# Sliding-window attention with sinks: a half-block's logits, values and products in a new order, and the low halves of sixteen weight panels on VectorE

## Chip, cores and metric

The kernel runs on one core of a Trainium2 chip. The metric is the device time of one execution in microseconds (us), as the median of several runs on one chip; lower is better. All data are float32. Where a large product is needed, each operand is split into a rounded high half and a low half, and three float32r matmuls (`mm3`: high by high, high by low, low by high) stand for one exact product.

## What is computed

The reference is a four-part network on 512 tokens of width 1024: a gated delta-rule mixer (stage a), attention with a 128-token window and sinks (stage b), a second mixer (stage m), and a product-key expert layer (stage p). The change lies in stage b alone. Cut to it:

```python
def swa_sink_mixer(h, w_in, q_gain, sinks, w_out, k_band, v_band, bias, mask):
    q, z = jnp.split(h @ w_in, 2, axis=-1)
    q = rms_norm(q.reshape(B, T, B_Q_HEADS, B_HD), q_gain) * (B_HD ** -0.5)
    q = q.reshape(B, nb, BLOCK, B_KV_HEADS, B_GROUP, B_HD)
    logits = jnp.einsum("bnqkgd,bnskd->bnkgqs", q, k_band) + bias
    logits = jnp.where(mask[None, :, None, None], logits, -jnp.inf)
    m = jnp.maximum(jnp.max(logits, axis=-1, keepdims=True), sink)
    p = jnp.exp(logits - m)
    probs = p / (jnp.sum(p, axis=-1, keepdims=True) + jnp.exp(sink - m))
    o = jnp.einsum("bnkgqs,bnskd->bnqkgd", probs, v_band)
    o = o.reshape(B, T, B_W) * jax.nn.silu(z)
    return o @ w_out
```

There are 4 key/value heads with 8 query heads each, head width 64, and 4 blocks of 128 tokens; a block of queries sees its own block of keys and the one before.

## The kernel before

Stage b works in four groups `g`, one for each key/value head. In a group, TensorE does two kinds of work.

The **attention** of the group is `block_b(k, s1, s2, g, n, b, ...)` for the four token blocks `n` and three parts `b`. Parts 0 and 1 take four heads each, a half. A half issues its logits (matmuls of line 901 into the PSUM tile `pl`), adds the bias and takes the row extreme on VectorE (line 904, into `lg` and `bm`), exponentiates on ScalarE (910), turns the result by TensorE transposes (917, into the PSUM tile `pt`), copies it to `PT` (919: the first copy of a half on ScalarE, the second on VectorE) and multiplies by the values (922, into `po`). Lines 907, 908 and 911 put the sink into the denominator `bden`. Part 2 divides by the denominators (883, 885), multiplies by the gate on GpSimd (887), turns the result (890) and splits it into `yh` and `yl` (212, 213).

The **projections** are the rest: `gates(g)` (16 steps of six matmuls into `pj`, then lines 805 and 806), the output projection `outputs(g - 1)` (16 steps of six, in the last group eight of twelve, each added to the residual `x` on VectorE, line 821: 56 adds) and `queries(g + 1)` (16 steps of six; after every fourth, `headnorm` makes `qn` on VectorE with lines 307, 206, 186 to 198 and 310, then line 794 turns it and line 795 copies it to `qT`). `weave` sorts the steps of both lists by their place in their own list. A scheduler then sets the order on each engine from this order and its own estimates of when an operand is ready. Every engine takes its instructions strictly in that order.

`Feed` streams the weight panels: a load on SyncE's queue, the high half on ScalarE (line 230 with a gain, 233 without), the low half on VectorE (231, two pieces) where there is a gain. A panel of the output projection (`wbo`, four for each group, 16 in all) has no gain; its low half is line 235, on GpSimd (`lo_on_pool=True`). Stage m has a `Feed` of its own with low halves on GpSimd.

PSUM holds two `pj`, two `pt`, three `pl` and one `po`. `yh` and `yl` have one buffer each: a group's first write to them waits until the output projection of the group before has read the old ones.

Of the kernel before, what the change touches and what calls it, by code (L numbers as in the profile page):

```python
# [7 lines left out]
F32 = mybir.dt.float32  # L8
# [4 lines left out]
AF = mybir.ActivationFunctionType  # L13
ALU = mybir.AluOpType
# [4 lines left out]
P = 128  # L19
T = 512  # L20
NT = 4
# [346 lines left out]
class Feed:  # L368


    def __init__(self, k, srcs, bufs):
        self.k, self.srcs, self.bufs = k, srcs, bufs
        self.raw, self.pans, self.done = [], [], 0

    def load(self, n):
# [5 lines left out]
    def prep(self, n):  # L381
        while len(self.pans) < min(n, len(self.srcs)):
            i = len(self.pans)
            self.load(i + 1)
            self.pans.append(self.k.halves(self.raw[i], bufs=self.bufs, gain=self.srcs[i][1], lo_on_pool=True))
            self.load(i + 3)

    def step(self, n=1):
# [8 lines left out]
def v4(t):  # L397
    return t.rearrange("p (n c) -> p n c", n=NT)
# [339 lines left out]
def stage_b(k):  # L738
    tc, nc, a = k.tc, k.nc, k.a
    with pool(tc, name="sb1", bufs=1) as s1:  # L740
        kT = s1.tile([P, 4, T], F32, name="kT")
# [39 lines left out]
        def queries(g, s2, pt, acc=None):  # L781
            d = gs[g]

            def use(t, p):
                if t == 0:
                    d["bias"] = s2.tile([P, 8, 256], F32, tag="bias", name="bias")
                    nc.sync.dma_start(d["bias"], bass.AP(k.brow.tensor, k.brow.offset + g * 8 * 384, [[1, P], [384, 8], [1, 256]]))
                    d["qT"] = s2.tile([P, 4, T], F32, tag="qT", name="qT", bufs=2)
                qn = s2.tile([P, 8, 64], F32, tag="qn", name="qn")
                k.headnorm(s2, p, qn, 8)  # L790
                q = pt()
                q2 = qn.rearrange("p (m j) c -> p m (j c)", j=2)
# [4 lines left out]
            return tiles_steps(k, feed, at["q", g], tiles, hh, hl, use, acc)  # L797

        def gates(g, s2):
            d = gs[g]  # L800
# [25 lines left out]
        with pool(tc, name="sb2", bufs=1) as s2:  # L826
# [23 lines left out]
                    f()  # L850
            with pool(tc, name="pb", bufs=2, space=PSUM) as k.pb:
                pt = lambda: k.pb.tile([P, 512], F32, tag="pt", name="pt")
                for g in range(4):
                    attend = [lambda n=n, b=b, g=g: block_b(k, s1, s2, g, n, b, gs[g], kT, V, sinkrow) for n in range(NT) for b in range(3)]
                    fill = gates(g, s2)
                    if g:
                        fill += outputs(g - 1, (0, 1), False) + outputs(g - 1, (2, 3), False)
                    if g < 3:
                        fill += queries(g + 1, s2, pt)
                        weave(attend, fill)  # L860
                        continue
                    o = outputs(3, range(4), True)
                    weave(attend[:9], fill)
                    weave(attend[9:], o[:4])
        for _, f in o[4:]:
            f()


def block_b(k, s1, s2, g, n, b, d, kT, V, sinkrow):

    nc = k.nc
    ts = slice(n * P, (n + 1) * P)

    s0, w = (3 - n) * P, P if n == 0 else 2 * P
    nst = w // P
    if b == 0:
        if n == 0:
            d["yh"], d["yl"] = (s1.tile([P, 4, T], F32R, tag=f"y{i}", name=f"y{i}") for i in "hl")
        d["po"] = k.pb.tile([P, 512], F32, tag="pv", name="po", bufs=1)
        d["den"] = k.sm.tile([P, 8], F32, tag="bden", name="bden")  # L880
    po, den = d["po"], d["den"]
    if b == 2:
        nc.vector.reciprocal(den, den)
        o = s2.tile([P, 512], F32, tag="ob", name="ob", bufs=2)
        nc.vector.tensor_tensor(out=o.rearrange("p (h c) -> p h c", h=8), in0=po.rearrange("p (h c) -> p h c", h=8),
                                in1=den.rearrange("p (h o) -> p h o", o=1).to_broadcast([P, 8, 64]), op=ALU.mult)
        nc.gpsimd.tensor_tensor(out=o, in0=o, in1=d["z"][n], op=ALU.mult)
        pt = v4(k.pb.tile([P, 512], F32, tag="pt", name="pt"))
# [3 lines left out]
        return  # L892
    hs = slice(4 * b, 4 * b + 4)
    sk = sinkrow[:, 8 * g + 4 * b : 8 * g + 4 * b + 4]
    lg = s2.tile([P, 4, 256], F32, tag="lg", name="lg", bufs=2)
    m = k.sm.tile([P, 4], F32, tag="bm", name="bm")
    for j in range(2):
        p = k.pb.tile([P, 512], F32, tag="pl", name="pl", bufs=3).rearrange("p (i s) -> p i s", i=2)
        js = slice(64 * j, 64 * j + 64)
        for i in range(2):  # L900
            nc.tensor.matmul(p[:, i, 0:w], d["qT"][js, 2 * b + i, ts], kT[js, g, s0 : s0 + w], start=True, stop=True)
        for i in range(2):
            h = 2 * i + j
            nc.vector.tensor_tensor_reduce(lg[:, h, 0:w], p[:, i, 0:w], d["bias"][:, 4 * b + h, 0:w], 1.0, sk[:, h : h + 1],
                                           ALU.add, ALU.min, m[:, h : h + 1])
    es = k.sm.tile([P, 4], F32, tag="bes", name="bes")
    nc.vector.tensor_tensor(out=es, in0=m, in1=sk, op=ALU.subtract)
    nc.scalar.activation(es, es, AF.Exp)
    for h in range(4):
        nc.scalar.activation(lg[:, h, 0:w], lg[:, h, 0:w], AF.Exp, scale=-1.0, bias=m[:, h : h + 1], accum_out=den[:, 4 * b + h : 4 * b + h + 1])  # L910
    nc.vector.tensor_tensor(out=den[:, hs], in0=den[:, hs], in1=es, op=ALU.add)
    PT = s2.tile([P, 8, P], F32, tag="PT", name="PT", bufs=2)
    for q in range(nst):
        pt = k.pb.tile([P, 512], F32, tag="pt", name="pt")
        for i in range(4):
            h, st = divmod(4 * q + i, nst)
            nc.tensor.transpose(pt[:, i * P : (i + 1) * P], lg[:, h, st * P : (st + 1) * P], k.ident)
        eng = nc.vector.tensor_copy if q else nc.scalar.copy
        eng(PT[:, 4 * q : 4 * q + 4, :], v4(pt))
    for h in range(4):  # L920
        for st in range(nst):
            nc.tensor.matmul(po[:, (4 * b + h) * 64 : (4 * b + h + 1) * 64], PT[:, h * nst + st, :],  # L922
                             V[:, s0 // P + st, g * 64 : (g + 1) * 64], start=(st == 0), stop=(st == nst - 1))

# [761 lines left out]
```

## Time and profile before

| | |
|---|---|
| runs (us) | 2825.43, 2817.9, 2822.9; median 2822.9 |
| profiled execution (us) | 2819.12, its span 2817.4 |
| busy share of the span | PE 95%, DVE 70%, ACT 40%, POOL 30% |
| mean granted TensorE clock | 0.984 |
| attention of stage b, first logits to the last output matmul | 689 to 1101 us of the span |

Engines: PE is TensorE, PEld its weight loads, DVE VectorE, ACT ScalarE, POOL GpSimd, SP SyncE. A matmul's end is modelled, so that matmuls that follow each other closely overlap in the profile: in an undisturbed run of them, one starts every 0.23 us and lasts 0.39 us. A gap shown before a matmul therefore is shorter than the time that PE lost there. "idle before, releaser" names what ended a gap. Line numbers are those of the kernel before.

### The profile page before, as it was taken

How to read it: one execution, taken by the hardware profiler on the slowest of the kernel's cores; microseconds unless marked ns; L12 is line 12 of the kernel's file. 1: busy time of each engine (PE TensorE's matmuls, PEld its weight loads, DVE VectorE, ACT ScalarE, POOL GpSimd, SP SyncE). 2: the span in 40 equal slices, each digit the busy share in tenths (PEclk: the TensorE clock that was granted, in tenths of full speed). 3: DMA queues.
4: the chain of work that ended last, by engine and by line, in shares of the span. 5: the costliest groups of instructions: out<-in, count | busy, mean ns of one | idle time of the engine just before them, and what ended most of it. 6: DMA issues, size and time to landing. Idle time of an engine off the chain costs nothing.

```text
span 2817.4 us, 39316 instructions
## 1 busy us (share of the span) xinstructions
PE 2686.6 (95%) x14291; PEld 2219.0 (79%) x14291; DVE 1966.2 (70%) x4283; ACT 1128.3 (40%) x2304; POOL 839.0 (30%) x609
## 2 busy tenths in 40 slices
PE   7999999989898989899998989899999999999999
PEld 5777777767676767677677788899888888888887
DVE  6566666665655656636646899986777877878886
ACT  5444444434443333333422245564333333333332
POOL 0100000000111032242123247864444444444441
PEclk9999999999999999999999989999999999999999
DMA  4111211121211222121013235557899999898996
GB/s 151 53 53 61 60 61 57 46 70 60 74 61 55 66 68 67 60 68 38 16 53 127 84 127 193 193 185 265 317 324 328 318 326 336 314 321 319 325 325 232
DMA packets 170462, 440.92 MB, mean 157 GB/s; under 512 B 13932, under 2 KB 79756, under 8 KB 168604
## 3 DMA queue, kind: packets, MB, share of 16 engines
q1 hardware_dynamic: 133404, 304.17, 32.8%
q0 software_dynamic: 36864, 134.23, 12.6%
q8 instruction: 113, 1.85, 0.3%
q14 instruction: 81, 0.66, 0.1%
HBM read 401.60 MB, written 36.75 MB: 156 GB/s over the span
## 4 chain that ended last, share of the span: by engine, by line
PE 68%; DVE 16%; issue 6%; ACT 5%; POOL 3%; DMA 2%; SPq 0%; ACTq 0%; DVEq 0%; POOLq 0%
PE pj L315 11%; PE pj L316 11%; PE pj L317 11%; PE acc L316 4%; PE acc L317 4%; PE acc L315 4%; ACT whio L233 2%; PE po L922 2%; PE pG L1644 1%; DVE x L1512 1%; DVE wloo L235 1%; DVE wlo L235 1%; PE po L316 1%; POOL o L1634 1%; PE po L315 1%
## 5 line engine op out<-in xcount | busy, mean ns | idle before, releaser
L315 PE MATMUL pj<-hThi,whi 128*128 128x384 f32 (+2 forms) x1664 | 603.6, 363 | 2.7 <-ACT hg L1390 2.0
L317 PE MATMUL pj<-hThi,wlo 128*128 128x384 f32 (+2 forms) x1664 | 593.5, 357 | 11.9 <-DVE wlo L235 11.9
L316 PE MATMUL pj<-hTlo,whi 128*128 128x384 f32 (+2 forms) x1664 | 598.0, 359 | 0.0
L317 PEld LDWEIGHTS pj<-hThi,wlo 128*128 128x128 f32 x1664 | 317.4, 191 | 33.9 <-DVE wlo L235 12.5
L315 PEld LDWEIGHTS pj<-hThi,whi 128*128 128x128 f32 x1664 | 317.2, 191 | 32.5 <-ACT hg L1390 2.7
L316 PEld LDWEIGHTS pj<-hTlo,whi 128*128 128x128 f32 x1664 | 317.7, 191 | 24.9 <-issue 1.3
L316 PE MATMUL acc<-wloo,Wh 128*128 128x512 f32 x768 | 302.9, 394 | 3.9 <-DVE wloo L235 2.5
L315 PE MATMUL acc<-whio,Wh 128*128 128x512 f32 x768 | 300.9, 392 | 0.5 <-ACT whio L233 0.4
L317 PE MATMUL acc<-whio,Wl 128*128 128x512 f32 x768 | 300.4, 391 | 0.0
L1503 POOL DMA_INDIRECT raw<-in_v_dram,ids x128 | 191.4, 1495 | 236.6 <-DVE wloo L235 114.7
L1503 POOL DMA_INDIRECT raw<-in_u_dram,ids x128 | 185.5, 1449 | 243.7 <-DVE wloo L235 115.0
L235 DVE TENSOR_TENSOR wlo<-raw,whi 128x1024 fp32r<-128x1024 f32 x128 | 161.1, 1258 | 77.8 <-ACT whi L233 77.8
L212 ACT CAST Wh<-W 128x384 fp32r<-128x384 f32 x128 | 65.7, 513 | 369.0 <-DVE W L1450 336.9
L233 ACT CAST whi<-raw 128x1024 fp32r<-128x1024 f32 x144 | 150.2, 1043 | 123.7 <-issue 88.2
L235 DVE TENSOR_TENSOR wloo<-raw,whio 128x1024 fp32r<-128x1024 f32 x128 | 156.8, 1225 | 51.5 <-ACT whio L233 51.5
L235 POOL TENSOR_TENSOR wlo<-wraw,whi 128x1024 fp32r<-128x1024 f32 x52 | 124.5, 2407 | 207.6 <-ACT whi L233 207.5
L316 PEld LDWEIGHTS acc<-wloo,Wh 128*128 128x128 f32 x768 | 144.2, 188 | 44.2 <-DVE wloo L235 16.5
L317 PEld LDWEIGHTS acc<-whio,Wl 128*128 128x128 f32 x768 | 144.2, 188 | 30.5
L315 PEld LDWEIGHTS acc<-whio,Wh 128*128 128x128 f32 x768 | 144.1, 188 | 29.4 <-ACT whio L233 1.4
L1512 DVE SCALAR_TENSOR_TENSOR x<-raw,act,x 128x1024 f32<-128x1024 f32 x128 | 163.8, 1280 | 1.0
L1507 DVE SCALAR_TENSOR_TENSOR raw<-raw,xt 128x1024 f32<-128x1024 f32 x128 | 154.0, 1219 | 0.0
L233 ACT CAST whi<-wraw 128x1024 fp32r<-128x1024 f32 x100 | 104.5, 1048 | 107.0 <-PE pj L316 70.0
(423 smaller groups left out, 5405.9 us busy)
## 6 DMA issues: line engine op xcount, KB each, us to landing
raw<-in_uT_dram SPq DMA_DIRECT2D x128, 512.0 KB
raw<-in_v_dram SPq DMA_DIRECT2D x128, 512.0 KB
wraw<-in_wa_dram SPq DMA_DIRECT2D x48, 512.0 KB
G<-stage SPq DMA_DIRECT2D x12, 2048.0 KB
Gt<-G SPq DMA_DIRECT2D x32, 768.0 KB
wraw<-in_wb_dram SPq DMA_DIRECT2D x32, 512.0 KB
wraw<-in_wmt_dram SPq DMA_DIRECT2D x20, 512.0 KB
H<-hg SPq DMA_DIRECT2D x48, 192.0 KB
```

Of the source, the lines that this page charges most:

```text
L212: self.nc.scalar.copy(hi, src)
L233: nc.scalar.copy(hi, raw)
L235: eng.tensor_tensor(out=lo, in0=raw, in1=hi.bitcast(F32), op=ALU.subtract)
L315: nc.tensor.matmul(out, wh, mh, start=first, stop=False)
L316: nc.tensor.matmul(out, wh, ml, start=False, stop=False)
L317: nc.tensor.matmul(out, wl, mh, start=False, stop=last)
L922: nc.tensor.matmul(po[:, (4 * b + h) * 64 : (4 * b + h + 1) * 64], PT[:, h * nst + st, :], V[:, s0 // P + st, g * 64 : (g + 1) * 64], star ...
L1503: nc.gpsimd.indirect_dma_start(out=g, out_offset=None, in_=src, in_offset=bass.IndirectOffsetOnAxis(ap=ids[:, j : j + 1], axis=0))
L1507: nc.vector.scalar_tensor_tensor(g, g, 1.0, xt0, op0=ALU.mult, op1=ALU.mult, accum_out=act[:, j : j + 1])
L1512: nc.vector.scalar_tensor_tensor(k.x[:, 0, :], g, act[:, j : j + 1], k.x[:, 0, :], op0=ALU.mult, op1=ALU.add)
L1634: nc.gpsimd.tensor_scalar(out=o1[:, n, :], in0=k.c["iota"], scalar1=selT[:, 1, cs][:, n : n + 1], scalar2=None, op0=ALU.is_equal)
L1644: nc.tensor.matmul(p[:, n * P : (n + 1) * P], o1[:, n, :], o0[:, n, :], start=True, stop=True)
```

## The change

Four things change, all in stage b.

1. `block_b` is called once for a group and returns five functions: `logits(u)`, `values(u)`, `products(u)`, `finish(n)` and `turn(n)`, with `u = 2n + b` for the eight halves. `values` is the transposes and copies, `products` the matmuls with the values. The list of attention steps puts `logits(u + 1)` ahead of `values(u)`, a `turn` of the block before between `values(u)` and `products(u)` for even `u`, and `finish` behind the products of odd `u`. Each is a step of its own for `weave`. The last turn of a group goes behind the first logits of the next.
2. In `queries`, the turn of `qn` is a step of its own, two projection steps behind the one that ends its tile; the last one goes into the next group's list.
3. `weave` of the last group is cut at another place: the four last output steps that are woven in lie beside `logits(6)` and what follows it.
4. Stage b's `Feed` gets `lo_on_pool=False`: the 16 low halves of `wbo` move from GpSimd to VectorE.

```diff
-    def __init__(self, k, srcs, bufs):
+    def __init__(self, k, srcs, bufs, lo_on_pool=True):
...
-        feed = Feed(k, srcs + wo(3), 6)
+        feed = Feed(k, srcs + wo(3), 6, lo_on_pool=False)
...
+            steps = []
+            for i, st in enumerate(tiles_steps(k, feed, at["q", g], tiles, hh, hl, use, acc)):
+                steps.append(st)
+                if i > 4 and i % 4 == 1:
+                    steps.append((0.2, lambda t=i // 4 - 1: turn(t)))
+            return steps + [(0.2, lambda: turn(NT - 1))]
...
-                    attend = [lambda n=n, b=b, g=g: block_b(k, s1, s2, g, n, b, gs[g], kT, V, sinkrow) for n in range(NT) for b in range(3)]
+                    L, V_, O_, F, T_ = block_b(k, s1, s2, g, gs[g], kT, V, sinkrow)
+                    attend = [lambda L=L: L(0)] + left
+                    for u in range(8):
+                        if u < 7:
+                            attend.append(lambda L=L, u=u: L(u + 1))
+                        attend.append(lambda V_=V_, u=u: V_(u))
+                        if u % 2 == 0 and u:
+                            attend.append(lambda T_=T_, u=u: T_(u // 2 - 1))
+                            if u == 4:
+                                cut = len(attend) + 1
+                        attend.append(lambda O_=O_, u=u: O_(u))
+                        if u % 2:
+                            attend.append(lambda F=F, u=u: F(u // 2))
+                    left = [lambda T_=T_: T_(NT - 1)]
...
                     if g < 3:
-                        fill += queries(g + 1, s2, pt)
-                        weave(attend, fill)
+                        qs = queries(g + 1, s2, pt)
+                        left.append(qs[-1][1])
+                        weave(attend, fill + qs[:-1])
                         continue
                     o = outputs(3, range(4), True)
-                    weave(attend[:9], fill)
-                    weave(attend[9:], o[:4])
+                    weave(attend[:cut], fill)
+                    weave(attend[cut:] + left, o[:4])
```

The arithmetic inside the five functions is that of before. In the changed kernel the lines are: logits 920 (was 901), bias and row extreme 923 (904), the denominator 926, 927 and 930 (907, 908, 911), exponentials 929 (910), transposes 940 (917), copies 942 (919), products 951 (922), division 956 and 958 (883, 885), gate 960 (887), turn 966 (890), query turn 797 (794), residual 830 (821).

What the scheduler makes of it shows at three places. The first is TensorE in group 0, at the first half of block 2. Before, its logits are `pl_6606` and `pl_6611`, and the exponentials of the same half (`lg_6604`) are turned five projection matmuls later:

```order
L901 MATMUL pl_6606<-kT_5592,qT_6067 128x256 x2
L901 MATMUL pl_6611<-kT_5592,qT_6067 128x256 x2
L315 MATMUL pj_6595<-whi_6267,hThi_5597 128x512
L316 MATMUL pj_6595<-wlo_6268,hThi_5597 128x512
L317 MATMUL pj_6595<-whi_6267,hTlo_5598 128x512
L315 MATMUL pj_6595<-whi_6267,hThi_5597 128x512
L316 MATMUL pj_6595<-wlo_6268,hThi_5597 128x512
L917 MATMUL pt_6625<-cst_71,lg_6604 128x128 x2
```

Now, `pl_6715` and `pl_6720` are the logits of the half after, and the transposes behind them read `lg_6616`, whose own logits were issued 30 projection matmuls, the eight transposes and the products of another half, and two turns earlier:

```order
L920 MATMUL pl_6715<-kT_5592,qT_6067 128x256 x2
L920 MATMUL pl_6720<-kT_5592,qT_6067 128x256 x2
L315 MATMUL pj_6705<-whi_6261,hThi_5597 128x512
L316 MATMUL pj_6705<-wlo_6262,hThi_5597 128x512
L317 MATMUL pj_6705<-whi_6261,hTlo_5598 128x512
L315 MATMUL pj_6705<-whi_6261,hThi_5597 128x512
L316 MATMUL pj_6705<-wlo_6262,hThi_5597 128x512
L317 MATMUL pj_6705<-whi_6261,hTlo_5598 128x512
L797 MATMUL pt_6739<-cst_71,qn_6677 128x128 x4
L940 MATMUL pt_6746<-cst_71,lg_6616 128x128 x4
```

So the distance from a half's logits to its transposes grew from five matmuls to a whole half's work.

The second is VectorE where group 0 passes into group 1, at the norm of the last tile of queries. Before:

```order
L307 TENSOR_REDUCE hss<-hsq 128x8
L206 TENSOR_SCALAR rv<-hss 128x8
L186 TENSOR_SCALAR rt<-rv 128x8
L188 TENSOR_SCALAR rr<-rt 128x8
L191 TENSOR_TENSOR rt<-rr 128x8
L192 SCALAR_TENSOR_TENSOR rt<-rt,rv 128x8
L193 SCALAR_TENSOR_TENSOR rr<-rt,rr 128x8
L213 TENSOR_TENSOR yl<-pt,yh 128x4x128
```

Now two low halves stand around the reduction, and the logits of the next group, with a denominator (930) that waits for ScalarE, stand ahead of the end of the norm:

```order
L235 TENSOR_TENSOR wlo<-wraw,whi 128x1024
L307 TENSOR_REDUCE hss<-hsq 128x8
L235 TENSOR_TENSOR wlo<-wraw,whi 128x1024
L206 TENSOR_SCALAR rv<-hss 128x8
L923 ISA lg,bm<-pl,bias,sinkrow 128x128
```

```order
L926 TENSOR_TENSOR bes<-bm,sinkrow 128x4
L193 SCALAR_TENSOR_TENSOR rr<-rt,rr 128x8
L195 SCALAR_TENSOR_TENSOR rt<-rr 128x8
L196 TENSOR_TENSOR rt<-rt,rv 128x8
L197 SCALAR_TENSOR_TENSOR rt<-rt 128x8
L930 TENSOR_TENSOR bden<-bden,bes 128x4
L198 SCALAR_TENSOR_TENSOR rr<-rt,rr 128x8
L310 TENSOR_TENSOR qn<-pj,rr 128x512
```

What moved: low halves from GpSimd into VectorE's queue, and four row extremes and two small steps of the denominator between the parts of the norm.

The third is GpSimd's queue in stage b. Before, low halves stand between the gate products:

```order
L769 COPY kd<-kv 128x512 x4
L887 TENSOR_TENSOR ob<-ob,sz 128x512 x4
L235 TENSOR_TENSOR wlo<-wraw,whi 128x1024 x2
L887 TENSOR_TENSOR ob<-ob,sz 128x512
L235 TENSOR_TENSOR wlo<-wraw,whi 128x1024 x2
L887 TENSOR_TENSOR ob<-ob,sz 128x512 x3
```

Now 14 gate products follow each other; the first two low halves of stage m come ahead of the last two products:

```order
L769 COPY kd<-kv 128x512 x4
L960 TENSOR_TENSOR ob<-ob,sz 128x512 x14
L235 TENSOR_TENSOR wlo<-wraw,whi 128x1024 x2
L960 TENSOR_TENSOR ob<-ob,sz 128x512 x2
L235 TENSOR_TENSOR wlo<-wraw,whi 128x1024 x2
L992 MEMSET V_9564 128x20
```

What moved: stage b's 16 low halves left this queue, and two of stage m came forward, into the end of the attention.

## Rows read from the trace of the kernel before

**Rows 1.** The page: the span, busy time by engine, and the slices.
```profile
span 2817.4 us, 39316 instructions
...
PE 2686.6 (95%) x14291; PEld 2219.0 (79%) x14291; DVE 1966.2 (70%) x4283; ACT 1128.3 (40%) x2304; POOL 839.0 (30%) x609
```

**Rows 2.** Busy time by stretch: length, PE, PEld, DVE, ACT, POOL, clock, DMA, GB/s.
```profile
688.00:1101.00 413.00, 383.64 (x2071) 296.30 (x2070) 232.84 (x685) 168.92 (x448) 63.60 (x35) 0.99 0.20 62
```

**Rows 3.** Waits of PE from 688 to 1101 us: total, times, longest.
```profile
PE pt L794 <- DVE bden L911: 9.1, 3, 4.4
PE pt L917 <- ACT lg L910: 7.5, 11, 1.1
PE pt L794 <- DVE qn L310: 6.6, 9, 3.7
PE pt L890 <- POOL ob L887: 4.3, 8, 0.5
PE pt L917 <- ACT PT L919: 1.2, 2, 0.6
PE pl L901 <- DVE bm L904: 0.3, 1, 0.3
```

**Rows 4.** Timeline of PE: one long wait at each change of group.
```profile
774.51 1.08 PE L794 MATMUL pt<-cst,qn 128*128 128x128 f32 x4 [3.71 <-DVE qn L310]
...
887.15 1.09 PE L794 MATMUL pt<-cst,qn 128*128 128x128 f32 x4 [4.35 <-DVE bden L911]
...
999.24 1.09 PE L794 MATMUL pt<-cst,qn 128*128 128x128 f32 x4 [4.37 <-DVE bden L911]
```

**Rows 5.** The four us behind each, and behind a short wait (columns as Rows 2).
```profile
774.00:778.00 4.00, 3.49 (x12) 2.90 (x13) 1.78 (x11) 2.33 (x10) 0.00 (x0) 0.58 0.23 91
887.00:891.00 4.00, 3.85 (x19) 3.60 (x19) 0.07 (x2) 1.17 (x2) 0.00 (x0) 0.63 0.35 118
999.00:1003.00 4.00, 3.76 (x16) 3.42 (x16) 0.16 (x2) 1.17 (x2) 0.00 (x0) 0.57 0.35 127
1034.00:1038.00 4.00, 3.14 (x21) 2.82 (x22) 2.74 (x6) 2.35 (x9) 2.42 (x2) 1.00 0.58 146
```

**Rows 6.** Timelines of POOL and DVE ahead of the first long wait.
```profile
767.21 4.73 POOL L235 TENSOR_TENSOR wlo<-wraw,whi 128x1024 fp32r<-128x1024 f32 x2
```
```profile
767.41 2.25 DVE L188 TENSOR_SCALAR rr<-rt 128x8 int32<-128x8 int32 x1
769.70 2.27 DVE L191 TENSOR_TENSOR rt<-rr 128x8 f32<-128x8 f32 x1
772.00 0.17 DVE L192 SCALAR_TENSOR_TENSOR rt<-rt,rv 128x8 f32<-128x8 f32 x1
```

**Rows 7.** Groups of DVE from 688 to 1101 us, by shape: busy, mean ns.
```profile
L907 DVE TENSOR_TENSOR bes<-bm,sinkrow 128x4 f32<-128x4 f32 x32 | 10.2, 318 | 0.8
...
L192 DVE SCALAR_TENSOR_TENSOR rt<-rt,rv 128x8 f32<-128x8 f32 x12 | 6.5, 540 | 0.3
L193 DVE SCALAR_TENSOR_TENSOR rr<-rt,rr 128x8 f32<-128x8 f32 x12 | 6.2, 515 | 0.3
...
L191 DVE TENSOR_TENSOR rt<-rr 128x8 f32<-128x8 f32 x12 | 4.1, 342 | 0.3
L188 DVE TENSOR_SCALAR rr<-rt 128x8 int32<-128x8 int32 x12 | 4.1, 342 | 0.2
...
L195 DVE SCALAR_TENSOR_TENSOR rt<-rr 128x8 f32<-128x8 f32 x12 | 2.0, 164 | 0.3
```

**Rows 8.** The page's groups: the same low half on DVE, in other stages, and on POOL.
```profile
L235 DVE TENSOR_TENSOR wlo<-raw,whi 128x1024 fp32r<-128x1024 f32 x128 | 161.1, 1258 | 77.8 <-ACT whi L233 77.8
...
L235 POOL TENSOR_TENSOR wlo<-wraw,whi 128x1024 fp32r<-128x1024 f32 x52 | 124.5, 2407 | 207.6 <-ACT whi L233 207.5
```

**Rows 9.** Timeline of a half near the end: logits, then the first transposes; matmuls; a turn.
```profile
1078.75 1.14 PE L901 MATMUL pl<-kT,qT 64*128 64x256 f32 x8
1079.82 0.50 PE L315 MATMUL pj<-whi,yh 128*128 128x512 f32 x1
...
1081.10 0.44 PE L917 MATMUL pt<-cst,lg 128*128 128x128 f32 x2 [0.55 <-ACT lg L910]
...
1087.68 0.66 PE L890 MATMUL pt<-cst,ob 128*128 128x128 f32 x4 [0.54 <-POOL ob L887]
...
1094.37 0.39 PE L315 MATMUL pj<-whi,yh 128*128 128x512 f32 x1
1094.60 0.39 PE L316 MATMUL pj<-wlo,yh 128*128 128x512 f32 x1
```

**Rows 10.** Waits of all engines from 688 to 1101 us: total, times, longest.
```profile
POOL wlo L235 <- ACT whi L233: 72.1, 10, 12.9
...
PEld pj L315 <- DVE x L821: 2.4, 8, 0.3
```

**Rows 11.** Groups of POOL and DVE from 688 to 1101 us: gate products and residual adds.
```profile
L887 POOL TENSOR_TENSOR ob<-ob,sz 128x512 f32<-128x512 f32 x16 | 20.6, 1288 | 304.4 <-DVE ob L885 304.4
...
L821 DVE TENSOR_TENSOR x<-x,pj 128x512 f32<-128x512 f32 x55 | 37.6, 684 | 25.0 <-PE pj L317 24.8
```

More of the change, by code (lines that the diff above doesn't have):

```diff
@@ L384, in prep @@
             self.load(i + 1)
-            self.pans.append(self.k.halves(self.raw[i], bufs=self.bufs, gain=self.srcs[i][1], lo_on_pool=True))
+            self.pans.append(self.k.halves(self.raw[i], bufs=self.bufs, gain=self.srcs[i][1], lo_on_pool=self.lo_on_pool))
             self.load(i + 3)
@@ L865, in stage_b, with block_b, where, logits @@
+                    weave(attend[cut:] + left, o[:4])
         for _, f in o[4:]:
             f()
-def block_b(k, s1, s2, g, n, b, d, kT, V, sinkrow):
+def block_b(k, s1, s2, g, d, kT, V, sinkrow):
     nc = k.nc
[L872 to L877, printed above, removed]
-            d["yh"], d["yl"] = (s1.tile([P, 4, T], F32R, tag=f"y{i}", name=f"y{i}") for i in "hl")
[L879 to L882, printed above, removed]
+    lgs, PTs, obs = {}, {}, {}
+    def where(u):
+        n, b = divmod(u, 2)
+        return n, b, (3 - n) * P, P if n == 0 else 2 * P
+    def logits(u):
+        n, b, s0, w = where(u)
+        if u == 0:
+            d["yh"], d["yl"] = (s1.tile([P, 4, T], F32R, tag=f"y{i}", name=f"y{i}") for i in "hl")
+        if b == 0:
+            d["den", n] = k.sm.tile([P, 8], F32, tag="bden", name="bden")
+        den, ts = d["den", n], slice(n * P, (n + 1) * P)
+        hs = slice(4 * b, 4 * b + 4)
+        sk = sinkrow[:, 8 * g + 4 * b : 8 * g + 4 * b + 4]
+        lgs[u] = lg = s2.tile([P, 4, 256], F32, tag="lg", name="lg", bufs=2)
+        m = k.sm.tile([P, 4], F32, tag="bm", name="bm")
+        for j in range(2):
+            p = k.pb.tile([P, 512], F32, tag="pl", name="pl", bufs=3).rearrange("p (i s) -> p i s", i=2)
+            js = slice(64 * j, 64 * j + 64)
+            for i in range(2):
+                nc.tensor.matmul(p[:, i, 0:w], d["qT"][js, 2 * b + i, ts], kT[js, g, s0 : s0 + w], start=True, stop=True)
+            for i in range(2):
+                h = 2 * i + j
+                nc.vector.tensor_tensor_reduce(lg[:, h, 0:w], p[:, i, 0:w], d["bias"][:, 4 * b + h, 0:w], 1.0, sk[:, h : h + 1],
+                                               ALU.add, ALU.min, m[:, h : h + 1])
+        es = k.sm.tile([P, 4], F32, tag="bes", name="bes")
+        nc.vector.tensor_tensor(out=es, in0=m, in1=sk, op=ALU.subtract)
+        nc.scalar.activation(es, es, AF.Exp)
+        for h in range(4):
+            nc.scalar.activation(lg[:, h, 0:w], lg[:, h, 0:w], AF.Exp, scale=-1.0, bias=m[:, h : h + 1], accum_out=den[:, 4 * b + h : 4 * b + h + 1])
+        nc.vector.tensor_tensor(out=den[:, hs], in0=den[:, hs], in1=es, op=ALU.add)
+    def values(u):
+        n, b, s0, w = where(u)
+        nst, lg = w // P, lgs.pop(u)
+        PTs[u] = PT = s2.tile([P, 8, P], F32, tag="PT", name="PT", bufs=2)
+        for q in range(nst):
+            pt = k.pb.tile([P, 512], F32, tag="pt", name="pt")
+            for i in range(4):
+                h, st = divmod(4 * q + i, nst)
+                nc.tensor.transpose(pt[:, i * P : (i + 1) * P], lg[:, h, st * P : (st + 1) * P], k.ident)
+            eng = nc.vector.tensor_copy if q else nc.scalar.copy
+            eng(PT[:, 4 * q : 4 * q + 4, :], v4(pt))
+    def products(u):
+        n, b, s0, w = where(u)
+        nst, PT = w // P, PTs.pop(u)
+        if b == 0:
+            d["po"] = k.pb.tile([P, 512], F32, tag="pv", name="po", bufs=1)
+        for h in range(4):
+            for st in range(nst):
+                nc.tensor.matmul(d["po"][:, (4 * b + h) * 64 : (4 * b + h + 1) * 64], PT[:, h * nst + st, :],
+                                 V[:, s0 // P + st, g * 64 : (g + 1) * 64], start=(st == 0), stop=(st == nst - 1))
+    def finish(n):
+        den = d["den", n]
@@ L887, in block_b, with turn @@
         nc.gpsimd.tensor_tensor(out=o, in0=o, in1=d["z"][n], op=ALU.mult)
+    def turn(n):
+        o, ts = obs.pop(n), slice(n * P, (n + 1) * P)
         pt = v4(k.pb.tile([P, 512], F32, tag="pt", name="pt"))
@@ L891, in block_b @@
         k.split(d["yh"][:, :, ts], d["yl"][:, :, ts], pt)
[L892 to L923, printed above, removed]
+    return logits, values, products, finish, turn
 def stage_m(k):
```

12 lines of the change are left out of this document (7 added, 5 removed).

## The prediction

> **What bounds the kernel now.** I read the page first [rows 1]: TensorE is busy for 95% of a span of 2817.4 us, and no other engine passes 70%. The kernel is bound by TensorE's own instructions; what a new order can give back is only the time in which TensorE stands still or runs at a lower clock. The change touches stage b alone, so the second view is that stage: in its 413 us from the first logits on, PE is busy for 383.64 and so shows about 29 us without work, while DVE is busy for 232.84 (56%) [rows 2]. The third view says what ended these gaps [rows 3]. The six rows sum to 9.1 + 7.5 + 6.6 + 4.3 + 1.2 + 0.3 = 29.0 us in 34 waits. All are waits of small transposes for a chain on other engines; none is for a load.
>
> Three things stand behind them, and the reader should see them apart.
>
> First, the change of group. Three waits of 3.71, 4.35 and 4.37 us [rows 4], 12.4 in all, stand before the turn of the last tile of queries. Behind each, the granted clock of a four us stretch reads 0.58, 0.63 and 0.57 [rows 5]: TensorE stood still, and then ran partly at the lower of its levels, 1.2 instead of 2.4 GHz. At full clock the stretches would have done 4 x (0.42 + 0.37 + 0.43) = 4.9 us more work.
>
> Why the wait is so long stands ahead of it [rows 6]. Two low halves run on POOL from 767.21 for 4.73 us. A step of the norm on 128x8 starts on DVE at 767.41 and lasts 2.25 us, the next 2.27, and the one after them 0.17. The last held step ends at 771.97, 0.03 us behind POOL's. Over the stage, steps that do like work have means of 540, 515, 342 and 342 ns where an unhindered one has 164 [rows 7]: (540 + 515 + 342 + 342 - 4 x 164) x 12 = 13.0 us, and the 32 steps of line 907 at 318 instead of 164 are 4.9 more. So DVE stands still for about 18 us, held by POOL.
>
> Second, a half's own chain. Its logits start at 1078.75, its first transposes at 1081.10 after a wait of 0.55 [rows 9]; only a couple of projection matmuls lie between, and the chain over DVE and ACT is longer. That is the row of 7.5 us.
>
> Third, the turn of a block waits for the gate product on POOL, 0.5 us each time [rows 3].
>
> A gap as shown is too short: matmuls start every 0.23 us and are drawn 0.39 long [rows 9], so each wait behind one hides another 0.16.
>
> **The change, part by part.** The sum is made against the profiled execution, 2819.12 us, which is 3.8 below the median of the three runs.
>
> *Logits a half ahead.* A half's transposes now come some 30 projection matmuls (30 x 0.23 = 6.9 us) and another half's work behind its logits. The chain needs 2.35 us to its first transposes [rows 9], and about 2 us more to its last exponential. Of the 8.7 us of both transpose rows [rows 3] I count 8 as gone, in 13 waits: 13 x 0.16 = 2.1 hidden us go with them. Products behind their copies: not one wait of products stands in [rows 3], so nothing.
>
> *Block turns later.* The turn stands about 7 us of PE's work behind the products that it needs, the chain is a division, a gate product of 1.29 us [rows 11] and some handing over. I count 3.8 of the 4.3 us as gone and keep one wait of 0.5 at the very end, where nothing is left to lay between; seven waits hide 1.1 more.
>
> *Query turns, and the low halves on DVE.* These go together, since both act on the 15.7 us of line 794 [rows 3]. Sixteen low halves on DVE at 1.258 us [rows 8] are 20.1 us of new work for DVE; the 18 us that it was held by POOL go. DVE's load thus stays where it was, at some 57%, and as an average it has room. In detail it is not free. For the last tile of a group, DVE's queue now has a low half on either side of the reduction, four row extremes and a denominator that waits for ACT's exponentials ahead of the last step of the norm. Added up, that is about 7.5 us from the end of the projection to `qn`, and PE has about 5.7 us of work to lay over it: logits, a turn and 18 projection matmuls. I take 1.5 us left for each of the three. The other nine waits are 15.7 - 12.4 = 3.3 us today; the second tile of a group has only 12 matmuls and one set of logits ahead of its turn (12 x 0.23 + 1.07 = 3.8 us), so I leave them at 3.5. Out of 15.7 stay 4.5 + 3.5 = 8, a gain of 7.7. Behind the longest wait for exponentials, 1.1 us [rows 3], the clock stayed at 1.00 [rows 5]; waits of about 4 us brought it down, so with waits of 1.5 the 4.9 us come back too.
>
> Here a rule of the Trainium skill can be weighed. The row [rows 6] shows a small step on DVE held to the end of POOL's instruction. Its page SBUF — State Buffer (SBUF: two separate sides) says that DVE and GpSimd share one pair of SBUF ports as an exclusive lock, held for a whole instruction, against instructions of DVE that run in a two-port mode or read two SBUF operands. The trace agrees in the 0.03 us above. The rule also speaks against part of this change, since a low half on DVE reads two SBUF operands and can itself hold, and be held by, the 16 gate products. By it up to 16 x 1.29 = 20.6 us of DVE's time could be lost again; they would mostly lie where a turn has its 7 us of cover.
>
> *What is added.* Low halves wait for ACT in DVE's queue, with row extremes, copies and the residual adds behind them, on which `pj`'s two buffers depend. The nearest row, PE's loads waiting for the residual, is 2.4 us [rows 10]; at best nothing is added (none of PE's waits is for a low half [rows 3], so a faster one wins nothing), at worst each of the 16 costs its full 1.26, 20 us. I take 2, nearest the row. At the end of the stage two low halves of stage m on POOL (2.4 us each [rows 8]) now run inside the last attention and hold DVE and the last gate products: between 0 and 2 x 2.4 = 4.8, I take 2. The loads keep their order and their count: nothing.
>
> *Sum.* 8 + 2.1 + 3.8 + 1.1 + 7.7 + 4.9 - 2 - 2 = 23.6 us. 2819.1 - 23.6 = 2795.5; as the runs' median may lie a little over a profiled execution, I say **2796**. All gaps, all hidden time (34 x 0.16 = 5.4) and the clock together are 39.3: the floor is 2780. Without the gain of line 794 and the clock, and with both additions at 4, it is 15.0 - 8 = 7.0: 2812.
>
> **The rivals.** *A, the group change stays.* The norm's queue, with ACT's exponentials in its middle, is as late as the lock made it: 12 us of waits and the lower clock remain, and only 15.0 - 4 = 11 us are won: 2808. For it speaks the order, in which the denominator stands ahead of the norm's last step; against it, that DVE is no longer held twice for 2.2 us.
>
> *B, no change that can be measured.* A measurement of this kernel tells 0.3%, 8.5 us, from nothing. The 56 residual adds share a queue with low halves and row extremes at a faster pace; if each made PE wait 0.35 us, 19.6 of the 23.6 us are given back: about 2815. Against it: an add is 0.68 us [rows 11], a step of six matmuls 1.4.
>
> *C, slower.* DVE takes over POOL's place behind ACT. POOL waited 72.1 us in ten waits for high halves [rows 10], which cost nothing on an idle engine; on DVE every row extreme stands behind such a wait. If all of it reached PE, the time would be 2795.5 + 72.1 = 2868. It decides from (23.6 + 8.5) / 72.1 = 45% of these waits on: from there the kernel is slower by over 0.3%; at 50% it is 2832. Against it: the scheduler puts the low half into DVE's order where it thinks it ready, while POOL's had nothing else to do but wait early.
>
> *D, the lock is not the cause.* If the long small steps come from elsewhere, the low halves are 20 us of DVE's time for nothing and the three long waits stay: this is A's time, 2808, and its chance is in A's. By the skill's rule the sum stays mine, without it A's.
>
> **How the numbers follow.** My forecast and its near surroundings (2784 to 2804) 0.62, A with D 0.21, B 0.10, C 0.05, and 0.02 for anything below 2782. The range takes in A and the lower bound, and leaves out most of B, and C: 2783 to 2812. Faster by over 0.3% is below 2814: my forecast, A, the odd low and a little of B, 0.86; within 0.3%: the most of B, 0.09; slower 0.05.
>
> **What would show it.** Right: from the first logits to stage m's first matmuls some 390 us instead of 413; no step of 128x8 on DVE over 1 us in the body of the stage; the wait of line 940 for exponentials under 1 us in all, that of 966 for the gate under 1; line 797 the largest row, under 9 us; the granted clock at 1.00 at each change of group; DVE's busy time in the stage within 5 us of 233. Wrong: waits of 4 us before line 797 and a clock near 0.6 behind them (A), many waits of `pj` for line 830 (B), long waits of line 235 on DVE for ACT with waits of line 940 behind them (C).

## The result, and the profile after

The changed kernel takes 2785.18 us (median of 4 runs, 2782.47 to 2787.56) where the kernel before, on the same chip, took 2821.12 (2817.9 to 2825.43): a ratio of 0.9872, 95% interval 0.9852 to 0.9892, or 36 us less. 2796 was predicted, in a range of 2783 to 2812.

The page of the changed kernel, to be laid beside [rows 1]:

```profile
span 2781.5 us, 39306 instructions
...
PE 2678.8 (96%) x14291; PEld 2222.2 (80%) x14291; DVE 1968.2 (71%) x4299; ACT 1127.4 (41%) x2304; POOL 810.0 (29%) x593
```

The matmuls are as many as before and PE is busy for about as long. Of the 35.9 us that the span is shorter, 28.1 are time in which PE shows no work; the other 7.8 are busy time of the same matmuls. Most of it comes from stage b: its first logits start at 688.94 us where they started at 689.01 before. The last output matmul of the stage starts at 1069.00 where it started at 1101.01 before: 32.0 us (timelines of PE, the kernel before first):

```profile
1101.01 0.40 PE L317 MATMUL pj<-whi,yl 128*128 128x512 f32 x1
```
```profile
1069.00 0.40 PE L317 MATMUL pj<-whi,yl 128*128 128x512 f32 x1
```

Busy time by stretch in the changed kernel (columns as in [rows 2]): the stage, and four us at one of the turns that open a new group and near the stage's end.

```profile
688.00:1066.00 378.00, 371.77 (x2057) 295.88 (x2057) 230.13 (x689) 166.80 (x446) 25.40 (x18) 1.00 0.22 68
...
871.00:875.00 4.00, 4.00 (x23) 3.07 (x23) 2.46 (x12) 2.45 (x9) 0.00 (x0) 1.00 0.32 124
1034.00:1038.00 4.00, 3.42 (x23) 2.44 (x22) 3.15 (x10) 3.91 (x7) 2.90 (x2) 1.00 0.00 0
```

Before, PE was without work for 29 of 413 us [rows 2]; now for 6.2 of 378. At a change of group it now works through: the granted clock of four us there reads 1.00, at 975 us as at 871, where [rows 5] had 0.58, 0.63 and 0.57. DVE is busy for 230.13 us, about as long as before, while POOL's 63.60 have fallen to 25.40. What is left of PE's waits in this stretch, beside the 34 waits of [rows 3]:

```profile
PE pt L797 <- DVE qn L310: 3.5, 5, 0.9
PE pt L940 <- DVE yl L213: 0.6, 1, 0.6
PE pj L315 <- DVE x L830: 0.6, 2, 0.3
PE pj L315 <- DVE sz L815: 0.3, 1, 0.3
PE pt L940 <- ACT qT L798: 0.3, 1, 0.3
PE po L951 <- ACT PT L942: 0.3, 1, 0.3
PE pl L920 <- DVE bm L923: 0.3, 1, 0.3
PE pt L966 <- ACT PT L942: 0.2, 1, 0.2
```

These are 6.1 us in 13 waits. So 29.0 - 6.1 = 22.9 us of waits are gone; with the 4.9 us of clock that the prediction read from [rows 5], and 21 waits fewer at its 0.16 hidden us, 3.4, that makes 31.2 of the 32.0 us. The other 3.9 us of the 35.9 lie behind stage b. In stage m, whose code the change doesn't touch, one row of waits went from 3.1 to 1.3 us (transposes of line 1034 for `fqn`) and one from 2.2 to 1.5; behind it the lead goes up and down by some us to the end. No cause of that has been found.

### The profile page after: what moved, and what is told of

It is laid out like the page before. It is cut to its first block, busy times and chain, and to the rows that moved or that the text cites. A ratio compares the mean times of both kernels' runs of the same rounds, so it can differ in the third digit from the quotient of the medians.

```text
span 2781.5 us, 39306 instructions
## 1 busy us (share of the span) xinstructions
PE 2678.8 (96%) x14291; PEld 2222.2 (80%) x14291; DVE 1968.2 (71%) x4299; ACT 1127.4 (41%) x2304; POOL 810.0 (29%) x593
## 4 chain that ended last, share of the span: by engine, by line
PE 72%; DVE 14%; ACT 5%; issue 5%; POOL 2%; DMA 2%; SPq 0%; ACTq 0%; DVEq 0%; POOLq 0%
PE pj L315 12%; PE pj L316 12%; PE pj L317 12%; PE acc L316 4%; PE acc L317 4%; PE acc L315 4%; PE pG L1690 2%; PE po L951 2%; ACT whio L233 2%; DVE x L1558 1%; DVE wloo L235 1%; PE pl L920 1%; PE po L316 1%; PE po L315 1%; PE po L317 1%
## 5 line engine op out<-in xcount | busy, mean ns | idle before, releaser
L1436 ACT ACTIVATE hg<-pj 128x384 f32<-128x384 f32 x128 | 62.6, 489 | 190.1 <-PE pj L317 190.1
```

The source lines that it names most:

```text
L1436: nc.scalar.activation(hg, p[:, 0:ND], AF.Gelu)
```

## The experiments

Two theories stood against each other. **The lock:** GpSimd's low halves held DVE's norm, and most of the gain is their move to DVE. **The distances:** the longer way between a half's logits, transposes and turns made room, and the move matters little. The runs are ratios to the kernel before on the same chip, each over five rounds. Where the text gives the length of stage b, it is that of a profiled execution, from the first logits to the last output matmul: 412.0 us before and 380.1 after.

### The low halves alone

The kernel before, with stage b's low halves on DVE and the lists of steps as they were:

```diff
-        feed = Feed(k, srcs + wo(3), 6)
+        feed = Feed(k, srcs + wo(3), 6, lo_on_pool=False)
```

(`Feed` also hands the argument through, as in the change.)

> The kernel before with one edit, the sixteen low halves of the output panels on DVE. Theory 'lock' (GpSimd's low halves hold DVE's small steps, and with them the norm of the last query tile): the three waits of 3.7 to 4.4 us at the changes of group shrink below 2 us, the clock stays at 1.00 there, the waits for exponentials of about 0.6 and 1.1 us behind a low half go too; 12.4 + 4.9 + some 3 us less at first sight, and with what is left of these waits 12 to 19 us faster than before: 2802 to 2809. Rival 'order' (the new order alone does it, DVE only gets 20 us of work): within 4 us of before, or slower by up to 5. No step of DVE on 128x8 over 0.5 us between 690 and 1060 us by 'lock'.

Measured: 2801.78 us, ratio 0.9926 (0.9913 to 0.9939): about 21 of the 36 us, a little more than the theory of the lock had forecast. PE's waits in the stage, beside [rows 3]:

```profile
PE pt L890 <- POOL ob L887: 4.9, 10, 0.5
PE pt L917 <- ACT lg L910: 4.1, 7, 1.0
PE pt L794 <- DVE qn L310: 3.2, 9, 0.5
```

The three waits of about 4 us are gone, and with them the low clock. Of the 8.7 us of waits before the transposes of line 917, 4.1 are left; those for the gate, which this kernel does nothing about, are still there. No small step of the norm's (lines 206 and 186 to 198) or of the denominator's (907, 911) lasts over 0.3 us in the stage.

This run doesn't measure the lock alone, though. The scheduler orders TensorE by its own estimates, and with the low halves on DVE it put the turn of the last query tile later. Timelines of PE and DVE at the first change of group, the kernel before first (its turn is the first line of [rows 4]):

```profile
770.41 0.40 PE L316 MATMUL pj<-wlo,hThi 128*128 128x512 f32 x1
```
```profile
773.28 0.39 PE L317 MATMUL pj<-whi,hTlo 128*128 128x512 f32 x1
773.60 0.71 PE L901 MATMUL pl<-kT,qT 64*128 64x128 f32 x6
774.24 0.66 PE L794 MATMUL pt<-cst,qn 128*128 128x128 f32 x4
```
```profile
766.23 0.69 DVE L307 TENSOR_REDUCE hss<-hsq 128x8 f32<-128x512 f32 x1 [0.46 <-ACT hsq L303]
773.68 0.69 DVE L310 TENSOR_TENSOR qn<-pj,rr 128x512 f32<-128x512 f32 x1
```
```profile
766.78 0.69 DVE L307 TENSOR_REDUCE hss<-hsq 128x8 f32<-128x512 f32 x1 [0.46 <-ACT hsq L303]
773.14 0.69 DVE L310 TENSOR_TENSOR qn<-pj,rr 128x512 f32<-128x512 f32 x1
```

Before, 2 projection matmuls stand between the new group's logits and the turn; here 12, and six more logits. From the reduction to the end of `qn` the norm took 8.14 us and takes 7.05: the holds are gone, but two low halves of 1.23 us now stand in its own queue. So some 1.1 us of the first wait of 3.71 went by the shorter norm and the rest by the later turn. At the other two changes the norm is 1.7 and 1.8 us shorter, and 24 instead of 16 projection matmuls start between the reduction and the turn. How much the move would bring with TensorE's order unchanged has not been run.

### The low halves back on GpSimd

The changed kernel with the one argument taken out (the edit above, reversed).

> The changed kernel with the sixteen low halves put back on GpSimd. Theory 'lock': steps of 128x8 on DVE of 2.2 us come back, and with them waits of PE of 3 us and more before the query turn at the three changes of group: 2795 to 2803, 10 to 18 us slower than the changed kernel. Rival 'order' (the turn's cover of some 5.7 us is enough): at most 4 us slower, 2785 to 2789, the DVE steps held but PE not waiting.

Measured: 2801.22 us, ratio 0.9922 (0.991 to 0.9935): 16 us slower than the changed kernel by the medians, 14 by the ratios. POOL and DVE beside a change of group (timelines), where the same hold stands as in [rows 6]:

```profile
867.61 4.75 POOL L235 TENSOR_TENSOR wlo<-wraw,whi 128x1024 fp32r<-128x1024 f32 x2 [1.50 <-ACT whi L233]
```
```profile
867.76 2.26 DVE L188 TENSOR_SCALAR rr<-rt 128x8 int32<-128x8 int32 x1
870.06 2.33 DVE L191 TENSOR_TENSOR rt<-rr 128x8 f32<-128x8 f32 x1
872.30 0.34 DVE L923 CUSTOM_DVE_ANT_0 lg<-pl,bias,sinkrow 128x128 f32<-128x128 f32 x1
```

In the profiled execution, the slowest of its six, PE's largest row of waits in the stage is again that of line 797 for `qn`, 7.1 us. The turns at the three changes of group wait 1.77, 2.22 and 2.21 us, where the changed kernel's don't wait; the 3 us and more that were forecast are not reached. Behind the last two the granted clock of four us falls to 0.66 and 0.57. This is the nearest to a measure of the hold: at the second change 20 projection matmuls start between reduction and turn in both kernels, and the norm takes 8.28 us here and 6.54 in the changed kernel.

The new orders alone bring 22 us, the low halves alone 21; together they bring 36. Stage b says the same: 392.7 us with the orders alone and 394.7 with the low halves alone, against 412.0 and 380.1. The two overlap by some 5 to 7 us: either of them shortens the same long waits at a change of group. Neither is the larger cause.

### GpSimd's low halves in four pieces

The kernel before, each low half of stage b as four instructions of 256 columns, still on GpSimd:

```diff
+        if lo_on_pool == 4:
+            for i in range(4):
+                cs = slice(256 * i, 256 * i + 256)
+                nc.gpsimd.tensor_tensor(out=lo[:, cs], in0=raw[:, cs], in1=hi[:, cs].bitcast(F32), op=ALU.subtract)
+            return hi, lo
...
-        feed = Feed(k, srcs + wo(3), 6)
+        feed = Feed(k, srcs + wo(3), 6, lo_on_pool=4)
```

> The kernel before with each of the sixteen low halves still on GpSimd, but as four instructions of 256 columns. Theory 'lock' (DVE is held to the end of the instruction that runs on GpSimd, not to the end of GpSimd's work): the longest held step of DVE falls from 2.25 us to about 0.65 us, each piece lets one step of DVE through, so a norm of ten steps crosses four to eight pieces instead of two: the long waits at the changes of group stay between 2 and 4 us and the time falls by 0 to 8 us. Rival 'bandwidth' (DVE is slowed in proportion while GpSimd works): no step changes its length by the pieces, waits and time as before within 3 us.

Measured: 2820.12 us, ratio 0.9998 (0.9987 to 1.0009). Here TensorE and DVE run the same instructions in the same order as before, so that only the hold differs. Timelines of POOL and DVE at the first change of group:

```profile
767.39 5.58 POOL L237 TENSOR_TENSOR wlo<-wraw,whi 128x256 fp32r<-128x256 f32 x8
```
```profile
767.58 0.58 DVE L188 TENSOR_SCALAR rr<-rt 128x8 int32<-128x8 int32 x1
768.20 0.67 DVE L191 TENSOR_TENSOR rt<-rr 128x8 f32<-128x8 f32 x1
768.90 0.67 DVE L192 SCALAR_TENSOR_TENSOR rt<-rt,rv 128x8 f32<-128x8 f32 x1
769.60 0.65 DVE L193 SCALAR_TENSOR_TENSOR rr<-rt,rr 128x8 f32<-128x8 f32 x1
770.17 0.68 DVE L213 TENSOR_TENSOR yl<-pt,yh 128x512 fp32r<-128x512 f32 x1
```

Two long holds have become eight short ones: 5.58 / 8 = 0.70 us is one piece, and each held step lasts to the end of one. A step is thus held until GpSimd's instruction ends, and one step passes between two of them. The norm still has seven held steps at this change of group and pays for nearly all the pieces one after the other: its turn waits 2.89 us instead of 3.71. Over the stage, the waits of line 794's turn fall from 15.7 to 12.9 us, but products now wait 2.6 us for copies; stage b is 3.3 us shorter, and the program's time no different that can be measured.

### One order undone at a time

In each of these kernels one part of the change is put back, all else stays as changed.

**Query turns** in their step again:

```diff
                 d["qn"] = qn
+                turn(t)
...
-                if i > 4 and i % 4 == 1:
-                    steps.append((0.2, lambda t=i // 4 - 1: turn(t)))
-            return steps + [(0.2, lambda: turn(NT - 1))]
+            return steps
...
-                        left.append(qs[-1][1])
-                        weave(attend, fill + qs[:-1])
+                        weave(attend, fill + qs)
```

> The changed kernel with the query turns put back into the step that ends their tile (the order given to the scheduler; it still places them itself). Theory 'cover': two steps of projection, 2.8 us, go from ahead of each of the twelve turns; the row of waits before line 797's turn grows from 3.5 us to 8 to 16 us: 2790 to 2798. Rival 'scheduler' (it puts the turn where it thinks the norm is ready, as it did before): within 3 us of the changed kernel, 2782 to 2788.

Measured: 2787.85 us, ratio 0.9875 (0.986 to 0.989), not told from the changed kernel; the rival came true. The scheduler hardly moved the turns that count: at the three changes of group 18, 22 and 22 projection matmuls start between reduction and turn, in the changed kernel 18, 20 and 20. So putting this part back costs next to nothing here. What a turn that really stood earlier would cost is not shown by it.

**Logits** directly ahead of their own half's values:

```diff
-                    attend = [lambda L=L: L(0)] + left
+                    attend = []
                     for u in range(8):
-                        if u < 7:
-                            attend.append(lambda L=L, u=u: L(u + 1))
+                        attend.append(lambda L=L, u=u: L(u))
+                        if u == 0:
+                            attend += left
```

> The changed kernel with each half's logits directly ahead of its own transposes again; all else stays (products, block turns and query turns late, low halves on DVE). Theory 'distance' (the half ahead is what took the waits for exponentials away): PE's row of transposes waiting for exponentials comes back with 4 to 9 us and some hidden time, 6 to 12 us slower than the changed kernel: 2791 to 2797. Rival 'free with the lock' (those waits came from DVE being held; the low halves on DVE took them away): at most 3 us slower, 2783 to 2788.

Measured: 2792.0 us, ratio 0.9894 (0.9879 to 0.9909), some 7 us slower by the medians. The intervals overlap a little, but each execution is slower than each of the changed kernel's, and stage b is 4.9 us longer. The waits of PE and of its loads for exponentials come back:

```profile
PE pt L941 <- ACT lg L930: 2.8, 7, 0.6
```
```profile
PEld pt L941 <- ACT lg L930: 12.5, 29, 1.0
```

All of PE's waits in the stage sum to 6.8 us, hardly more than the 6.1 of the changed kernel; the loss is rather to be looked for in the loads.

**Block turns** right behind the division and the gate:

```diff
-                        if u % 2 == 0 and u:
-                            attend.append(lambda T_=T_, u=u: T_(u // 2 - 1))
...
                         if u % 2:
-                            attend.append(lambda F=F, u=u: F(u // 2))
-                    left = [lambda T_=T_: T_(NT - 1)]
+                            attend.append(lambda F=F, T_=T_, u=u: (F(u // 2), T_(u // 2)))
+                    left = []
```

> The changed kernel with each block's turn directly behind its division and gate product. Theory: 16 waits of about 0.5 us for GpSimd's gate product come back, each hiding 0.16 more: 6 to 10 us slower than the changed kernel, 2791 to 2795. Rival 'scheduler' (it lays projection matmuls ahead of the turn by itself): within 3 us, 2782 to 2788.

Measured: 2794.48 us, ratio 0.9912 (0.9897 to 0.9928): 9 us slower by the medians, the largest of the four orders, though its interval meets those of logits and products; stage b is 7.3 us longer. The wait for the gate stands there again, and longer than in [rows 3]:

```profile
PE pt L964 <- POOL ob L958: 5.8, 7, 1.4
```

**Products** in one step with their copies, the block's turn ahead of both:

```diff
-                        attend.append(lambda V_=V_, u=u: V_(u))
...
-                        attend.append(lambda O_=O_, u=u: O_(u))
+                        attend.append(lambda V_=V_, O_=O_, u=u: (V_(u), O_(u)))
```

> The changed kernel with the products with the values in one step with their transposes and copies (the block turn ahead of both). No wait of products stood in the trace of the kernel before, so by my reckoning this part brought nothing: within 3 us of the changed kernel, 2782 to 2788. Rival 'copy' (with the rest gone, the copy becomes the late one): products waiting for copies in 28 pairs at 0.3 to 0.5 us, 8 to 14 us slower: 2793 to 2799.

Measured: 2790.08 us, ratio 0.9884 (0.9867 to 0.99). By the medians that is 5 us slower, between the two theories; the intervals overlap, and stage b is 3.8 us longer. In the trace the loads of `po` wait for the copies, and the projections longer for the residual:

```profile
PEld po L950 <- ACT PT L941: 6.2, 18, 0.8
```
```profile
PE pj L315 <- DVE x L830: 2.6, 3, 1.1
```

In the changed kernel those were 1.8 and 0.6 us. The prediction had called this part worth nothing, since PE has no such wait in [rows 3]; its loads had one in the kernel before:

```profile
PEld po L922 <- ACT PT L919: 3.5, 14, 0.5
```

### Further: stage m's low halves too

The changed kernel, with the low halves of stage m's panels on DVE as well (`lo_on_pool=False` in stage m's `Feed`).

> The changed kernel with stage m's low halves on DVE as well. In the changed kernel's stage m DVE is held some 25 us by GpSimd, and PE shows 15.7 us of waits, 5.4 of them for a held step of a norm and 3.4 and 2.4 for others near held steps. By 'lock': 4 to 10 us faster than the changed kernel, 2775 to 2781, no step of DVE held there. Rival 'load' (36 low halves at 1.23 us are 44 us for DVE, more than the 25 it gets back): 0 to 8 us slower, 2785 to 2793.

Measured: 2779.52 us, ratio 0.9839 (0.9823 to 0.9855). It is faster than both kernels, than the changed one by some 6 us: the two intervals just touch, but each of its executions is below each of the changed kernel's. DVE's steps in stage m (groups by shape, the changed kernel first):

```profile
L198 DVE SCALAR_TENSOR_TENSOR rr<-rt,rr 128x8 f32<-128x8 f32 x9 | 5.6, 625 | 0.3
...
L188 DVE TENSOR_SCALAR rr<-rt 128x8 int32<-128x8 int32 x9 | 3.6, 402 | 0.2
```
```profile
L188 DVE TENSOR_SCALAR rr<-rt 128x8 int32<-128x8 int32 x9 | 1.5, 167 | 0.1
...
L198 DVE SCALAR_TENSOR_TENSOR rr<-rt,rr 128x8 f32<-128x8 f32 x9 | 1.5, 164 | 0.2
```

Two of PE's waits go with the hold (one for `rr`, from 5.4 to 1.3 us, and one of 3.4 for `so`).

**The first four of them on GpSimd.** In the list of waits of that run one of 7.7 us for `xn` stood out, and I took it for stage m's start.

```diff
-            self.pans.append(self.k.halves(self.raw[i], bufs=self.bufs, gain=self.srcs[i][1], lo_on_pool=self.lo_on_pool))
+            self.pans.append(self.k.halves(self.raw[i], bufs=self.bufs, gain=self.srcs[i][1], lo_on_pool=i < 4 if self.lo_on_pool == 4 else self.lo_on_pool))
```

(Stage m's `Feed` gets `lo_on_pool=4`.)

> The kernel with both stages' low halves on DVE, except the first four of stage m, which GpSimd makes. With all of them on DVE, TensorE stood 7.7 us at stage m's start behind a norm whose DVE step came after two low halves (2.34 us together). Theory 'the queue': that wait came because DVE had low halves ahead of the norm; without them it is about 3 us or less, at most one or two steps of DVE at the end of stage b are held for up to 2.3 us, and the time is 2775 (2771 to 2779). Theory 'the chain': stage m's start waits for reductions, norms and transposes whoever makes the low halves; the wait stays at 5 us or more and the time at 2780. If the two low halves' hold on the norm costs as much as it saves, the start reads as in the changed kernel, 5.4 us or so for a held step, and the time is 2780 too.

Measured: 2777.97 us, ratio 0.9839 (0.9826 to 0.9853), the same as the run before. The wait is still 7.9 us, and both theories were about the wrong place: it stands at the start of stage p, behind stage m, and the kernel before and the changed kernel have it too (timelines of PE, before first):

```profile
1492.01 1.94 PE L264 MATMUL pt<-cst,xn 128*128 128x128 f32 x8 [7.99 <-DVE xn L254]
```
```profile
1457.61 1.94 PE L264 MATMUL pt<-cst,xn 128*128 128x128 f32 x8 [7.83 <-DVE xn L254]
```

A wait in a list by stage has to be looked up in the timeline before a theory is built on it. Nothing follows from this run on the first four panels but that it makes no difference that can be measured.

## Why the prediction was right, and where it was too small

- **The bound** was right: PE's matmuls are the same, and the gain is waits and clock.
- **The hold** was read rightly, and rival D falls: in the run with pieces the held steps take the length of the pieces, and with the low halves on DVE the long steps are gone. What the move saves the norm at a change of group is less than the hold, though: the two holds of [rows 6] cost some 2.25 + 2.27 - 2 x 0.17 = 4.2 us, and two low halves in the norm's own queue cost 2.5. In the run with the low halves alone the norm is 1.1 to 1.8 us shorter, and more of the three long waits went by the later turn that the scheduler chose. The prediction had named the hold alone as the reason of these waits.
- **Line 794 was the mis-sized term.** Of 15.7 us, 8 were to stay, 4.5 of them at the three changes of group; 3.5 stayed, and none at a change. The gain is 12.2 us, not 7.7. I had the norm's chain at 7.5 us against 5.7 of PE's work. In the trace, at the second change, the tile's last projection matmul ends at 863.76 + 0.40 = 864.16, `qn` (310) at 870.68 + 0.69 = 871.37, and the turn starts at 871.60 without a wait. The denominator (930), which I had put ahead of the norm's end, comes behind it here and at the third change; at the first it stands ahead and waits for nothing:

```profile
864.83 0.69 DVE L307 TENSOR_REDUCE hss<-hsq 128x8 f32<-128x512 f32 x1 [1.89 <-ACT hsq L303]
...
870.68 0.69 DVE L310 TENSOR_TENSOR qn<-pj,rr 128x512 f32<-128x512 f32 x1
871.28 0.15 DVE L930 TENSOR_TENSOR bden<-bden,bes 128x4 f32<-128x4 f32 x1
```
```profile
863.76 0.40 PE L317 MATMUL pj<-whi,hTlo 128*128 128x512 f32 x1
...
871.60 0.66 PE L797 MATMUL pt<-cst,qn 128*128 128x128 f32 x4
```

  The chain took 871.37 - 864.16 = 7.2 us and was sized well. What was too small is the work of PE over it: 871.60 - 864.16 = 7.4 us instead of 5.7. I had counted the 18 projection matmuls behind the new group's logits; six more (some 1.4 us) stand ahead of these logits, behind the tile's last one, and some logits of the half after stand ahead of the turn. So rival A falls, and the clock's 4.9 us came back, as the prediction had it. It had this gain as a pair, later turns and the move. The runs don't part the pair: the turns' edit undone left them nearly in place, and with the low halves back on GpSimd the turn still waits 7.1 + 2.2 = 9.3 us instead of 15.7.
- **The additions** were put at 4 us of new waits. Those that PE now has (rows of lines 940, 315 and 951) sum to 0.6 + 0.6 + 0.3 + 0.3 + 0.3 = 2.1. DVE's low halves wait only 5.6 us for ACT in all, where POOL's waited 72.1 [rows 10]. Rival B falls with the 0.6 us that PE now waits for the residual (line 830), C with this row of the changed kernel:

```profile
DVE wlo L235 <- ACT whi L233: 5.6, 8, 1.4
```

- **Logits ahead and block turns** were sized well by their waits: 8 and 3.8 forecast, 8.7 and 4.3 - 0.2 = 4.1 gone. The 8.7 are not the half ahead's alone, though: the move by itself takes 4.6 of them. Undone alone the two cost 7 and 9 us; the turn more than the 4.9 forecast. In the new order a turn put at once waits up to 1.4 us instead of 0.5, but PE's waits in that run sum to only 3.3 us more than the changed kernel's, and the rest of the loss is not accounted for.
- **Products behind their copies: nothing** is not borne out: 5 us by the medians, an amount that the overlapping intervals leave open, and longer waits in the trace. I had looked for a wait of PE in [rows 3], and the longer waits stand with PE's loads and with the projections' wait for the residual.
- In all, the terms came to 23.6 us and stage b gave 32.0: 4.5 from line 794, 1.9 from the additions, 1.0 from logits and turns, and about 1 unassigned. The last 3.9 lie behind the stage; the prediction had nothing for them, and they brought the time nearer to the low end of its range.
- Of the signs named beforehand, one failed: "no step of 128x8 on DVE over 1 us". There are two of 1.28 us, told of below. And from the first logits to stage m's first matmuls it is some 381 us, where "some 390" was named.

## What to carry to other kernels

Look for small steps on VectorE that last many times their usual time, and then for what GpSimd runs beside them. Work on GpSimd was not free here, since a chain that TensorE waits for ran on VectorE meanwhile: sixteen low halves cost 16 x 1.29 us on VectorE, and their move, with the order that the scheduler then chose, brought 21 us. Cutting GpSimd's work into smaller instructions won nothing that could be measured, since the chain has about as many steps as there were pieces. Where a scheduler sets the order, an edit in one engine's queue can move another engine's instructions: compare the orders of all engines before a gain is put down to the edit's own mechanism. And when parts of a change shorten the same waits, neither the gain of one alone nor the loss without it is its share; run both.

## What the runs showed of the hardware

**A held step ends with GpSimd's instruction, whatever its own size.** 128x8 steps that were held from near the start of GpSimd's instruction lasted 2.25 to 2.40 us beside instructions of 2.4 us, 0.58 to 0.74 beside pieces of 0.70, and 1.28 beside a gate product of 1.29. The last is in the changed kernel, ahead of its longest wait (POOL, then DVE, then PE):

```profile
837.94 1.29 POOL L960 TENSOR_TENSOR ob<-ob,sz 128x512 f32<-128x512 f32 x1 [21.23 <-DVE rv L206]
```
```profile
837.98 1.28 DVE L186 TENSOR_SCALAR rt<-rv 128x8 uint32<-128x8 uint32 x1
```
```profile
841.75 0.63 PE L797 MATMUL pt<-cst,qn 128*128 128x128 f32 x4 [0.92 <-DVE qn L310]
```

The same three stand 103.6 us later (a hold of 1.28 at 941.52, a wait of 0.91). They and one low half on DVE, which took 2.23 us instead of 1.23 beside a gate product (at 760.43), are the little that came true of the 20.6 us that the gate products might have cost. **Not every step is held.** In the run with four pieces, line 213, which reads PSUM, took its usual 0.68 us between held steps. Row extremes, which read PSUM too, kept their pace while two low halves of stage m ran at the end of the changed kernel's stage b (POOL, then DVE):

```profile
1035.10 4.76 POOL L235 TENSOR_TENSOR wlo<-wraw,whi 128x1024 fp32r<-128x1024 f32 x2 [12.78 <-ACT whi L233]
```
```profile
1036.74 0.47 DVE L923 CUSTOM_DVE_ANT_0 lg<-pl,bias,sinkrow 128x256 f32<-128x256 f32 x1
```

The Trainium skill, on its page SBUF — State Buffer (SBUF: two separate sides), calls the pair of ports that VectorE and GpSimd share an exclusive lock for a whole instruction, taken by a step of VectorE in a two-port mode or with two operands in SBUF. The lengths above agree with it, and so do the steps with a PSUM operand, which ran free. Lines 186 and 188 have one operand and were held; in what mode they run no row shows.
